# RWKV-7 / mLSTM / MoE block: dependent ScalarE and VectorE instructions a dense step apart

## The chip, the cores and the metric

The kernel runs on one core of one Trainium2 chip. The metric is the device time of one execution in microseconds. The core's engines run side by side, each in the order in which its instructions were written: TensorE (PE; its weight loads are shown as PEld), VectorE (DVE), ScalarE (ACT), GpSimd (POOL) and SyncE (SP). They wait for each other through semaphores. The order on every engine is the order in which the Python code below issues the instructions; nothing reorders them afterwards.

## What is computed

One decoder block over 256 tokens of width 2048, in float32:

```python
u = x @ w_in[i]                                    # 2048 -> RWKV-7 | mLSTM | merge gates
u_r, u_m, u_g = _split(u, [RWKV_COLS, MLSTM_COLS, GATE_COLS])
y_r = _rwkv7_mixer(u_r, ...)                       # 16 heads of 64, state updated token by token
y_m = _mlstm_mixer(u_m, ...)                       # 8 heads, chunks of 128 tokens
g_r, g_m = _split(u_g + b_gate[i], [d, d])
mix = (sigmoid(g_r) * (y_r @ w_br[i]) + sigmoid(g_m) * (y_m @ w_bm[i])) @ w_out[i]
x = _layer_norm(ALPHA * x + mix, ln1_w[i], ln1_b[i])
moe = _hier_moe(x, ...)                            # 4 groups x 8 experts, top-1 group, top-2 experts
ple = sigmoid(x @ w_pg[i]) * (p[i] @ w_ple[i])
x = _layer_norm(ALPHA * x + moe + ple, ln2_w[i], ln2_b[i])
```

In the RWKV mixer the projections are mixed with the previous token's, decay and gates come from low-rank products, and each head's output is normalised (centred, divided by its root mean square deviation), scaled, added to a bonus and gated. In the mLSTM mixer q and k pass a causal convolution of four taps and a SiLU, and each head's output is normalised and gated by a sigmoid.

## The kernel before

**The dense stage** is everything from x @ w_in to @ w_out. Its work is a list of units: a block of 256 (or 512) output columns, summed over k. `run` goes through the units in dense steps. In a step of kind "T", TensorE multiplies two k-blocks of weights with x. To keep float32 accuracy in the faster fp32r format, every weight is split into a rounded part and a rest: ScalarE copies (L217) and VectorE subtracts (L218). TensorE then does four pairs of a 512-column matmul (L282) and a 256-column one (L283). In a step of kind "N" (mLSTM's v and w_out) it does six 512-column matmuls (L290 to L292). The split of a step is issued three steps ahead (`AHEAD = 4`), into four buffers, and the loads of raw weights on SP's queue follow the splits. A unit accumulates in a pair of PSUM banks (`bank2`, two such pairs).

The steps are numbered here from 0. A w_in unit of kind "T" has 8 steps and one of kind "N" 16; a w_br or w_bm unit has 4. The order is: low-rank columns, RWKV's r, k, v in four groups of four heads mixed with the merge gates' units, q and k (`evac_qk`), v (`evac_mv`), the output gate (`evac_o`), w_br (steps 336 to 367), w_bm (to 399), w_out (to 463).

**Evacuations and mixers** fill the other engines beside the dense matmuls. Both are Python generators. After each dense step `advance` lets the first evacuation in the queue run to its next `yield`, and then the first mixer to its next one; a mixer's `yield n` lets it rest until n steps have passed. So what a generator issues between two yields stands together in one dense step, behind that step's split and dense matmuls. An evacuation starts in the last step of its unit. It begins with `total`: ScalarE copies the second half of the accumulators (L345) and VectorE adds the first (L346); then come the token shift (`shift_mix`, `shift_chunks`), the convolution (`evac_qk`) or a gate.

`rwkv(g)` is the mixer of a group of four heads. Its prologue has two table loads of ScalarE (square root L433, exponential L436) and two reciprocals (L440, L442). Then a triangular inverse in five levels, and a loop over four chunks j of 64 tokens: the state's part of the chunk is subtracted (L562 to L566), L573 multiplies with the inverse, the state is updated (L583 to L587), the output is summed (L595 to L599). `centre(tb)` takes the mean of two chunks' outputs away on VectorE (L635 to L637) and squares them on ScalarE (L638); `squares(tb)` sums the squares on VectorE (L630). In the tail come the square root (L607), reciprocal and product (L609, L611), the transposes (L615), scaling on ScalarE (L619), bonus and gate on VectorE (L621, L622), and the split of the result (L624, L625).

`mlstm` follows when the last v unit is evacuated. Its first loop has one head per round in a pipeline (`copy_out`, `finish`, `scores` in one step; `spread`, `scores_late`, `values` in the next: L784 makes what L789 multiplies). Its second loop scales two heads per step on ScalarE (L835), transposes the two before (L844), multiplies with the output gate (L848) and splits (L851, L852). `evac_br`, `evac_bm` and `evac_out` take the results of w_br, w_bm and w_out; `evac_out` adds the residual (L916), transposes (L925) and feeds the router.

**The MoE stage** streams the experts' weights (about 2 MB per load) and is not touched.

Of the kernel before, what the change touches and what calls it, by code (L numbers as in the profile page):

```python
# [116 lines left out]
def hybrid_block(ctx: ExitStack, tc: tile.TileContext, xt, xp, vec, cst, sel8, rows, ln1c, pt, w_lora, w_rkv, w_qk,  # L117
# [224 lines left out]
    def total(p_, dst=None):  # L342
# [3 lines left out]
        dve.tensor_tensor(dst, dst, p_[:, :n, :256], op=OP.add)  # L346
        return dst

    def shift_mix(dst, src, mu, omu):
        act.activation(dst, src, AF.Identity, bias=0.0, scale=omu)  # L350
        dve.scalar_tensor_tensor(dst[:, 1:], src[:, :255], mu, dst[:, 1:], op0=OP.mult, op1=OP.add)
# [28 lines left out]
    def evac_mixed(g, w):  # L380

        name, lock, old = (("mu_r", "zr", g - 1), ("mu_k", "zr", g - 1), ("mu_v", "zv", g - 2))[w]
        dst = (zr, zk, zv[:, g % 2])[w]

        def f(p_):
            t = total(p_)
            yield
            while free[lock] < old:
                yield
            for c in range(2):  # L390
                (shift_chunks if w == 2 else shift_mix)(dst[:, :, c] if w == 2 else dst[:, c], t[:, c],
                                                        *vm(name, 2 * g + c))
                yield
            if w == (1 if g else 2):
                mixers.append(rwkv(g))
        return f

    def rwkv(g):
# [159 lines left out]
        for j in range(4):  # L558
            if j:
                ps_, py = bank(), (bank(), bank())  # L560
                for c, q in quads:
                    mm(py[q][half[c], :64], PR[half[q], c, j, 1, :], S0[half[q], c, :], start=True, stop=True)  # L562
                for q, c in quads:
                    mm(ps_[half[q], 64 * c:64 * c + 64], PR[half[q], c, j, 0, :], S0[half[q], c, :], start=True,
                       stop=True)
                dve.tensor_tensor(Xs[:, :, j, :], Xs[:, :, j, :], ps_[:, :128].rearrange("p (c n) -> p c n", c=2),  # L566
                                  op=OP.add)
                for q in range(2):
                    act.activation(yN[:, j, q, :], py[q][:, :64], AF.Copy)
                yield 1  # L570
            pn = (bank(), bank())
            for c, q in quads:
                mm(pn[q][half[c], :64], Gm[half[q], j, c, :], Xs[half[q], c, j, :], start=True, stop=True)  # L573
            for q in range(2):
                act.activation(nS[:, j, q, :], pn[q][:, :64], AF.Copy, scale=-1.0)
            if 0 < j < 3:
                dve.tensor_tensor(S1, S0, scal[:, :, j:j + 1].to_broadcast([128, 2, 64]), op=OP.mult)
            yield 1
# [20 lines left out]
                dve.tensor_tensor(yN[:, j], yN[:, j], pY, op=OP.add)  # L599
            else:  # L600
                act.activation(yN[:, j], pY, AF.Copy)
            if j % 2:
                centre(j // 2)
            yield 1
            if j % 2:
                squares(j // 2)
        act.activation(rstd, rstd, AF.Sqrt, scale=1.0 / 64, bias=eps_r)  # L607
        yield 1
        dve.reciprocal(rstd, rstd)  # L609
# [8 lines left out]
        for c in range(2):  # L618
            act.activation(yT[:, c].rearrange("p (j n) -> p j n", j=4), pyc[:, c], AF.Identity,  # L619
                           scale=v_("lnx_w", 2 * g + c), bias=v_("lnx_b", 2 * g + c))  # L620
        dve.tensor_tensor(yT, yT, bon, op=OP.add)  # L621
        dve.tensor_tensor(yT, yT, gg, op=OP.mult)  # L622
        hi, lo_ = (yr[:, 2 * g:2 * g + 2, n] for n in range(2))
        act.activation(hi, yT, AF.Copy)  # L624
        dve.tensor_tensor(lo_, yT, hi.bitcast(FT), op=OP.subtract)  # L625
        free["y"] = g
        yield 1

    def squares(tb):
        dve.tensor_reduce(rstd[:, tb], ysq[:, tb], axis=AX.X, op=OP.add)  # L630

    def centre(tb):
        y = yN[:, 2 * tb:2 * tb + 2].rearrange("p j q n -> p (j q) n")
        m = mean[:, tb]
        dve.tensor_reduce(m, y, axis=AX.X, op=OP.add)  # L635
        dve.tensor_scalar(m, m, -1.0 / 64, None, op0=OP.mult)
        dve.tensor_tensor(y, y, m[:, :, None].to_broadcast([128, 4, 64]), op=OP.add)  # L637
        act.activation(ysq[:, tb], y, AF.Square)  # L638

# [27 lines left out]
    def evac_qk(u):  # L669
        w = u // 2  # L670
        dst = (qT, kT)[w]

        def f(p_):
            t = total(p_)
            yield
            while free["zr"] < 3:
                yield
            for c in range(2):
                src, i = t[:, c], 2 * u + c
                d = dst[:, i % 4]  # L680
                act.activation(d, src, AF.Identity, scale=v_("cw3", i), bias=v_("conv_b", i))
                for j in range(1, 4):
                    dve.scalar_tensor_tensor(d[:, j:], src[:, :256 - j], v_("cw%d" % (3 - j), i), d[:, j:],
                                             op0=OP.mult, op1=OP.add)
                yield
            if u % 2:
                act.activation(sgq, dst, AF.Tanh, scale=0.5)
                dve.scalar_tensor_tensor(dst, sgq, 1.0, dst, op0=OP.add, op1=OP.mult)
        return f

# [13 lines left out]

    def evac_o(u):
        def f(p_):
            t = total(p_, so[:, 2 * u:2 * u + 2])
            yield
            act.activation(t, t, AF.Tanh, scale=0.5)
            dve.tensor_scalar(t, t, 0.5, 0.5, op0=OP.mult, op1=OP.add)  # L710
            free["o"] = u
        return f

    def mlstm():
# [93 lines left out]
        for h in range(11):  # L808
# [12 lines left out]
            if 0 < h < 9:  # L821
                values(h - 1)
            if h < 9:
                yield 1
        act.activation(hrstd, hmv[:, :, :, 1], AF.Sqrt, bias=eps_m)
        dve.reciprocal(hrstd, hrstd)
        dve.scalar_tensor_tensor(hmean, hmv[:, :, :, 0], -1.0, hrstd, op0=OP.mult, op1=OP.mult)
# [3 lines left out]
        for h2 in range(5):  # L831
# [3 lines left out]
                        act.activation(hN[:, tb, h], hN[:, tb, h], AF.Identity, scale=hrstd[:, tb, h:h + 1],  # L835
                                       bias=hmean[:, tb, h:h + 1])
            if h2 == 0:
                yield 1
                continue
            h2 -= 1  # L840
            py = bank()
# [8 lines left out]
            hi, lo_ = (ym[0][:, 2 * h2:2 * h2 + 2, n] for n in range(2))  # L850
            act.activation(hi, yTm, AF.Copy)  # L851
            dve.tensor_tensor(lo_, yTm, hi.bitcast(FT), op=OP.subtract)  # L852
            yield 1

    def evac_gate(u):
        def f(p_):
            t = total(p_, gates[u // 8][:, 2 * u % 16:2 * u % 16 + 2])  # L860
            yield
            for c in range(2):
                act.activation(t[:, c], t[:, c], AF.Tanh, scale=0.5, bias=v_("b_gate", 2 * u + c))
                yield
        return f
# [3 lines left out]

    def evac_br(u):  # L870
        def f(p_):
            gt, t = gates[0][:, 2 * u:2 * u + 2], total(p_)
            yield
            dve.scalar_tensor_tensor(gt, gt, 1.0, t, op0=OP.add, op1=OP.mult)
        return f

    def evac_bm(u):
        def f(p_):
            if u == 0:
                mix.extend(_carve(big(i, FR), 0, 16, 256) for i in (4, 5))  # L880
                tmp[0] = M.rearrange("p (a t) -> p a t", t=256)[:, 0::3]
            t = total(p_)
            yield
            gr, gm = (fl(a[:, 2 * u:2 * u + 2]) for a in gates)
            dve.scalar_tensor_tensor(gates[1][:, 2 * u:2 * u + 2], gates[1][:, 2 * u:2 * u + 2], 1.0, t, op0=OP.add,
                                     op1=OP.mult)
# [1 line left out]
            yield  # L888
            hi = fl(mix[0][:, 2 * u:2 * u + 2])
            act.activation(hi, gr, AF.Copy, scale=0.5)  # L890
            dve.scalar_tensor_tensor(fl(mix[1][:, 2 * u:2 * u + 2]), gr, 0.5, hi.bitcast(FT), op0=OP.mult,
                                     op1=OP.subtract)
        return f
# [15 lines left out]
    def evac_out(u):  # L909
        def f(p_):  # L910
# [3 lines left out]
            for tb in range(2):  # L914
# [2 lines left out]
                                         op1=OP.add)  # L917
                if u < 3:
                    dve.bn_stats(stats[:, tb, u], x1[:, tb, o])
                yield  # L920
            for half in range(2):
                pz, k0 = held[1 + (2 * u + half) % 3], 4 * u + 2 * half
# [942 lines left out]
```

## Time and profile before

| | |
|---|---|
| median of three runs | 1820.55 us (1819.59 to 1824.2) |
| the profiled execution | 1823.52 us, of which the span from first to last instruction is 1821.8 |
| busy over the span | PE 1599.6 us (88%), PEld 1081.0 (59%), DVE 794.0 (44%), ACT 607.4 (33%) |
| last dense step | ends at about 851 us |
| memory traffic | 541.38 MB by DMA, 297 GB/s in the mean |

A row of the timeline holds the start and the length in us, the engine, the line, the operation, output and inputs by tile name (B, M, R, C, V, sm in SBUF, dps and mps in PSUM), shapes, and in brackets the engine's idle time before it with the instruction that ended it. Matmuls overlap, and their ends are modelled; start-to-start times are surer than busy times. A wait "X <- Y" is idle time of X's engine, ended by Y.

### The profile page before, as it was taken

Reading aid. Unit: us, or ns where it says so; the run is one execution under the profiler, and the core shown is the slowest. Engines: PE = TensorE matmul, PEld = TensorE weight load, DVE = VectorE, ACT = ScalarE, POOL = GpSimd, SP = SyncE. Lnnn points to the kernel's source line nnn. Section 1 sums busy time; section 2 is a strip of 40 time slices with the busy share of each in tenths; the row PEclk is TensorE's granted clock in tenths of the full one; section 3 lists DMA queues with packets and bytes.
Section 4 is the critical chain, followed back from the end, with each engine's and each line's share of the span. In section 5 each row is a group of like instructions: output and inputs, shape, how many; then the busy total and the mean of one; then the engine's idle time right before and its main releaser. Section 6 shows DMA issues by size and latency. Waiting matters only on the chain. (4 is left out here: it accounts for less than half of the span.)

```text
span 1821.8 us, 34784 instructions
## 1 busy us (share of the span) xinstructions
PE 1599.6 (88%) x14339; PEld 1081.0 (59%) x14339; DVE 794.0 (44%) x1664; ACT 607.4 (33%) x1179; POOL 26.6 (1%) x38
## 2 busy tenths in 40 slices
PE   7999999999989999997879787897797878987876
PEld 6787787877868778875447444455364433433332
DVE  5675756757765777854331121220211313221206
ACT  5645645646455465544111111111111111111122
POOL 0000000000000000000000000000000000000002
PEclk9999999999999999998899998899899998998888
DMA  7443434434336347975899999999999999999997
GB/s 243 157 153 116 157 129 134 151 117 141 127 105 196 106 139 240 362 228 222 353 426 427 426 425 426 393 425 426 426 426 426 426 426 396 385 427 425 426 426 323
DMA packets 68073, 541.38 MB, mean 297 GB/s; under 512 B 7740, under 2 KB 12108, under 8 KB 42016
## 3 DMA queue, kind: packets, MB, share of 16 engines
q1 hardware_dynamic: 67152, 537.33, 74.4%
q8 instruction: 142, 2.33, 0.5%
q0 software_dynamic: 720, 1.25, 0.3%
q14 instruction: 59, 0.48, 0.1%
HBM read 536.44 MB, written 2.36 MB: 296 GB/s over the span
## 5 line engine op out<-in xcount | busy, mean ns | idle before, releaser
L282 PE MATMUL dps<-B,B 128*128 128x512 f32 x1456 | 538.7, 410 | 12.1 <-ACT B L217 9.3
L283 PE MATMUL dps<-B,B 128*128 128x256 f32 x1456 | 411.0, 282 | 4.8 <-DVE B L218 4.7
L218 DVE TENSOR_TENSOR B<-B,B 128x512 fp32r<-128x512 f32 (+1 forms) x464 | 312.3, 683 | 188.9 <-ACT B L217 184.0
L1355 PE MATMUL dps<-B,B 128*32 128x256 f32 x3968 | 260.6, 418 | 87.9 <-DMA B<-in_w_gate_dram 39.9
L217 ACT ACTIVATE B<-B 128x512 fp32r<-128x512 f32 (+1 forms) x464 | 283.7, 623 | 161.8 <-PE dps L282 62.5
L282 PEld LDWEIGHTS dps<-B,B 128*128 128x128 f32 x1456 | 275.6, 189 | 84.5 <-ACT B L217 11.7
L283 PEld LDWEIGHTS dps<-B,B 128*128 128x128 f32 x1456 | 277.0, 190 | 12.3 <-DVE B L218 10.0
L1355 PEld LDWEIGHTS dps<-B,B 128*32 128x32 f32 x3968 | 139.3, 119 | 214.3 <-DMA B<-in_w_gate_dram 50.8
L1361 DVE SCALAR_TENSOR_TENSOR M<-M,dps 128x128 f32<-128x128 f32 x31 | 8.9, 289 | 401.9 <-ACT M L1360 401.9
L1719 ACT ACTIVATE B<-mps 32x512 f32<-32x512 f32 x120 | 70.6, 588 | 191.4 <-PE mps L1376 190.3
L1376 PE MATMUL mps<-B,M 128*32 128x512 f32 x992 | 127.4, 653 | 5.9 <-issue 2.7
L1170 PE MATMUL mps<-B,B 128*128 128x206 f32 (+1 forms) x640 | 112.8, 337 | 0.6 <-DVE B L1159 0.3
L1360 ACT ACTIVATE M<-dps 128x128 f32<-128x128 f32 x31 | 8.6, 278 | 309.1 <-PE dps L1355 309.1
L1170 PEld LDWEIGHTS mps<-B,B 128*128 128x128 f32 x640 | 110.6, 190 | 1.6 <-DVE B L1159 0.6
L1376 PEld LDWEIGHTS mps<-B,M 128*32 128x32 f32 x992 | 31.5, 118 | 83.5 <-issue 76.9
L290 PE MATMUL dps<-B,B 128*128 128x512 f32 x192 | 76.1, 396 | 2.7 <-ACT B L217 2.7
L292 PE MATMUL dps<-B,B 128*128 128x512 f32 x192 | 75.3, 392 | 0.9 <-DVE B L218 0.8
L291 PE MATMUL dps<-B,B 128*128 128x512 f32 x192 | 74.9, 390 | 0.0
L1427 DVE TENSOR_TENSOR B<-mps,V 128x512 f32<-128x512 f32 x31 | 21.4, 692 | 90.8 <-PE mps L1423 90.8
L1396 PE MATMUL mps<-B 128*128 128x512 f32 (+1 forms) x128 | 56.7, 595 | 0.7 <-ACT B L1719 0.7
L1183 DVE SCALAR_TENSOR_TENSOR C<-C,mps 128x412 f32<-128x412 f32 (+1 forms) x10 | 5.8, 581 | 102.6 <-PE mps L1175 102.6
L1182 ACT ACTIVATE C<-mps 128x412 f32<-128x412 f32 (+1 forms) x10 | 5.1, 512 | 129.9 <-issue 70.4
(465 smaller groups left out, 1585.0 us busy)
## 6 DMA issues: line engine op xcount, KB each, us to landing
B<-in_w_up_dram SPq DMA_DIRECT2D x62, 2048.0 KB, 24.5
B<-in_w_gate_dram SPq DMA_DIRECT2D x62, 2048.0 KB, 21.8
B<-in_w_down_dram SPq DMA_DIRECT2D x60, 2048.0 KB, 22.9
B<-in_w_gt_dram SPq DMA_DIRECT2D x64, 512.0 KB, 3.7
B<-in_w_rkv_dram SPq DMA_DIRECT2D x48, 512.0 KB, 3.9
B<-in_w_pg_dram SPq DMA_DIRECT2D x10, 1854.0 KB, 30.3
B<-in_w_out_dram SPq DMA_DIRECT2D x32, 512.0 KB, 3.7
B<-in_w_qk_dram SPq DMA_DIRECT2D x16, 512.0 KB, 4.0
```

The lines of the kernel that those rows point to most:

```text
L217: act.activation(h, src, AF.Copy)
L218: dve.tensor_tensor(wl[i % 4][:, :w], src, h.bitcast(FT), op=OP.subtract)
L282: mm(pt_[:, c], h[:, w], x.rearrange("p a t -> p (a t)"), start=k == 0, stop=False)
L283: mm(pt_[:, c, :256], l[:, w], x[:, 0], start=False, stop=k == nk - 1)
L290: mm(o, mh[:, ts_], h, start=first, stop=False)
L291: mm(o, ml[:, ts_], h, start=False, stop=False)
L292: mm(o, mh[:, ts_], l, start=False, stop=last)
L1170: mm(pp[:, tb], x1T[0][:, k, tb * 128:tb * 128 + 128], w[:, k, :n], start=k == 0 and tb == 0, stop=k == 15 and tb == 1)
L1355: mm(pu[32 * j:32 * j + 32].rearrange("p (a f) -> p a f", a=2), xs[:, 4 * q + k, :], w[:, :, k, 128 * j:128 * j + 128], start=q == QS[0] a ...
L1376: mm(pd[32 * j:32 * j + 32, :], hT_[:, 32 * c:32 * c + 32], w[:, c % 2, 512 * j:512 * j + 512], start=c == 0, stop=c == 3)
L1396: mm(pz, SWT[p0:p1, tb * 128:tb * 128 + 128], yq[p0:p1, o], start=True, stop=True)
L1719: act.activation(yq[32 * i:32 * i + 32, 512 * j:512 * j + 512], pd[32 * j:32 * j + 32, :], AF.Copy)
```

## The change

`total_slow` takes the place of `total` in all evacuations but the low-rank ones: the copy, a yield, the addition, a yield. In the other generators yields are put in wherever one of ScalarE and VectorE makes something that the other uses, or pieces are moved to a later yield. `centre` loses its last line, which becomes `square`. An mLSTM head's round takes three steps (1 + 2) instead of two, and the second mLSTM loop gives each pair of heads two steps.

```diff
+    def total_slow(p_, dst=None):
+        dst = tmp[0] if dst is None else dst
+        n = dst.shape[1]
+        act.activation(dst, p_[:, :n, 256:], AF.Copy)
+        yield
+        dve.tensor_tensor(dst, dst, p_[:, :n, :256], op=OP.add)
+        yield
+        return dst
...
         def f(p_):
-            t = total(p_)
-            yield
+            t = yield from total_slow(p_)
...
                     act.activation(yN[:, j, q, :], py[q][:, :64], AF.Copy)
+                if j == 2:
+                    centre(0)
                 yield 1
...
+            if j == 2:
+                square(0)
+            if j == 3:
+                squares(0)
...
-            if j % 2:
-                centre(j // 2)
             yield 1
-            if j % 2:
-                squares(j // 2)
+        centre(1)
+        yield 1
+        square(1)
+        yield 1
+        squares(1)
+        yield 1
         act.activation(rstd, rstd, AF.Sqrt, scale=1.0 / 64, bias=eps_r)
...
+        yield 1
         dve.tensor_tensor(yT, yT, bon, op=OP.add)
         dve.tensor_tensor(yT, yT, gg, op=OP.mult)
+        yield 1
         hi, lo_ = (yr[:, 2 * g:2 * g + 2, n] for n in range(2))
         act.activation(hi, yT, AF.Copy)
+        yield 1
         dve.tensor_tensor(lo_, yT, hi.bitcast(FT), op=OP.subtract)
...
-        act.activation(ysq[:, tb], y, AF.Square)
+
+    def square(tb):
+        act.activation(ysq[:, tb], yN[:, 2 * tb:2 * tb + 2].rearrange("p j q n -> p (j q) n"), AF.Square)
...
                 act.activation(sgq, dst, AF.Tanh, scale=0.5)
+                yield
                 dve.scalar_tensor_tensor(dst, sgq, 1.0, dst, op0=OP.add, op1=OP.mult)
...
-            t = total(p_, so[:, 2 * u:2 * u + 2])
+            t = yield from total_slow(p_, so[:, 2 * u:2 * u + 2])
+            act.activation(t, t, AF.Tanh, scale=0.5)
             yield
-            act.activation(t, t, AF.Tanh, scale=0.5)
...
             if h < 9:
-                yield 1
+                yield 2
...
             if h2 == 0:
-                yield 1
+                yield 2
...
             dve.tensor_tensor(lo_, yTm, hi.bitcast(FT), op=OP.subtract)
-            yield 1
+            yield 2
...
             hi = fl(mix[0][:, 2 * u:2 * u + 2])
             act.activation(hi, gr, AF.Copy, scale=0.5)
+            yield
...
                 if u < 3:
                     dve.bn_stats(stats[:, tb, u], x1[:, tb, o])
+                yield
+            if u < 3:
                 yield
```

Written out, the order on VectorE in the first RWKV group, from the end of chunk j = 1 (L599, after the change L613) to the wait of chunk 2 for L573's operand (L566, after it L574), is this before:

```order
L587 SCALAR_TENSOR_TENSOR B_67<-mps,B_67 128x64 x2
L599 TENSOR_TENSOR B_67<-B_67,mps 128x128
L635 TENSOR_REDUCE B_67<-B_67 128x4
L636 TENSOR_SCALAR B_67<-B_67 128x4
L637 TENSOR_TENSOR B_67<-B_67 128x256
L218 TENSOR_TENSOR B_70<-B_69,B_70 128x512
L351 SCALAR_TENSOR_TENSOR B_63<-R,V,B_63 128x255
L630 TENSOR_REDUCE B_67<-B_67 128x4
L566 TENSOR_TENSOR B_66<-B_66,mps 128x2x64
```

and after (L654 to L656 are centring, L360 the token shift's second half):

```order
L601 SCALAR_TENSOR_TENSOR B_67<-mps,B_67 128x64 x2
L613 TENSOR_TENSOR B_67<-B_67,mps 128x128
L218 TENSOR_TENSOR B_70<-B_69,B_70 128x512
L360 SCALAR_TENSOR_TENSOR B_63<-R,V,B_63 128x255
L574 TENSOR_TENSOR B_66<-B_66,mps 128x2x64
L654 TENSOR_REDUCE B_67<-B_67 128x4
L655 TENSOR_SCALAR B_67<-B_67 128x4
L656 TENSOR_TENSOR B_67<-B_67 128x256
```

Centring has moved behind the operand of L573, and the row sum L630 out of this piece.

On ScalarE, the end of the last RWKV group (L619 scaling, L624 split of the result) and the conv's gate (L687), where the v units begin, stand like this before:

```order
L681 ACTIVATE B_63<-R,V 128x256
L619 ACTIVATE B_67<-mps,V 128x256 x2
L624 ACTIVATE B_65<-B_67 128x2x256
L217 ACTIVATE B_70<-B_69 128x512
L687 ACT_TABLE_LOAD
L687 ACTIVATE B_63<-B_63 128x1024
L217 ACTIVATE B_70<-B_69 128x512 x13
```

After the change the gate (L707) stands in the chunk loop, between the state's products (L577, L585), and Square (L659) later:

```order
L701 ACTIVATE B_63<-R,V 128x256
L217 ACTIVATE B_70<-B_69 128x512
L707 ACTIVATE B_63<-B_63 128x1024
L577 ACTIVATE B_67<-mps 128x64 x2
L217 ACTIVATE B_70<-B_69 128x512
L585 ACTIVATE B_66<-mps 128x64 x2
L659 ACTIVATE B_67<-B_67 128x256
```

and the tail's end, with L635 for the scaling, L642 for the split of the result and L717 for the v unit's copy, is spread among the splits:

```order
L717 ACTIVATE B_64<-dps 128x4x128
L635 ACTIVATE B_67<-mps,V 128x256 x2
L217 ACTIVATE B_70<-B_69 128x512
L717 ACTIVATE B_64<-dps 128x4x128
L217 ACTIVATE B_70<-B_69 128x512
L642 ACTIVATE B_65<-B_67 128x2x256
L217 ACTIVATE B_70<-B_69 128x512 x14
```

The scaling and the result's copy no longer stand in one piece, and no table load follows them.

More of the change, by code (lines that the diff above doesn't have):

```diff
@@ L673, in f @@
         def f(p_):
-            t = total(p_)
-            yield
+            t = yield from total_slow(p_)
             while free["zr"] < 3:
@@ L852, in mlstm @@
             dve.tensor_tensor(lo_, yTm, hi.bitcast(FT), op=OP.subtract)
-            yield 1
+            yield 2
     def evac_gate(u):
         def f(p_):
-            t = total(p_, gates[u // 8][:, 2 * u % 16:2 * u % 16 + 2])
-            yield
+            t = yield from total_slow(p_, gates[u // 8][:, 2 * u % 16:2 * u % 16 + 2])
             for c in range(2):
@@ L871, in f @@
         def f(p_):
-            gt, t = gates[0][:, 2 * u:2 * u + 2], total(p_)
-            yield
+            gt, t = gates[0][:, 2 * u:2 * u + 2], (yield from total_slow(p_))
             dve.scalar_tensor_tensor(gt, gt, 1.0, t, op0=OP.add, op1=OP.mult)
@@ L881, in f @@
                 tmp[0] = M.rearrange("p (a t) -> p a t", t=256)[:, 0::3]
-            t = total(p_)
-            yield
+            t = yield from total_slow(p_)
             gr, gm = (fl(a[:, 2 * u:2 * u + 2]) for a in gates)
```

## Prediction

> **What bounds the kernel now.** I read the busy time on both sides of the last dense step, then TensorE's waits in the dense stage, then the timeline at each wait. First, by stretches (bounds and length in us; busy PE, PEld, DVE, ACT, POOL; granted clock, DMA share, GB/s):
>
> ```profile
> 25.00:851.00 826.00, 798.40 (x6448) 644.02 (x6446) 549.77 (x1049) 447.77 (x860) 4.51 (x12) 1.00 0.49 162
> 851.00:877.00 26.00, 17.54 (x170) 9.26 (x174) 12.28 (x67) 7.92 (x14) 0.00 (x0) 0.67 0.80 341
> 877.00:1821.00 944.00, 768.83 (x7669) 415.68 (x7661) 220.20 (x525) 140.76 (x291) 17.67 (x15) 0.92 0.98 415
> ```
>
> Up to 851 us TensorE is busy 97% of the time and the DMA engines half: the dense stage, where the whole diff lies, goes at TensorE's pace. From 877 us the DMA share is 0.98: the experts' weights stream in, and no edit touches that. The stream fills tiles that the dense stage gives back, so I let a microsecond saved before 851 move the end by a microsecond.
>
> TensorE's pace in an undisturbed step:
>
> ```profile
> 59.87 0.39 PE L282 MATMUL dps<-B,B 128*128 128x512 f32 x1
> 60.10 0.28 PE L283 MATMUL dps<-B,B 128*128 128x256 f32 x1
> 60.22 0.39 PE L282 MATMUL dps<-B,B 128*128 128x512 f32 x1
> ```
>
> A pair takes 0.35 us from start to start, a step of four pairs 1.39. ScalarE and VectorE make the split weights (L217, L218) three steps ahead; TensorE stops only when a split is later than that, or a mixer's operand is late. All its waits from 30 to 850 us (in total, times, longest):
>
> ```profile
> PE mps L573 <- DVE B L566: 5.9, 4, 2.2
> PE dps L283 <- DVE B L218: 4.7, 12, 1.1
> PE mps L615 <- DVE B L611: 4.7, 4, 1.2
> PE dps L290 <- ACT B L217: 2.7, 2, 1.8
> PE dps L282 <- ACT B L217: 1.9, 5, 0.4
> PE mps L925 <- DVE B L916: 1.9, 3, 1.0
> PE mps L789 <- DVE B L784: 1.7, 1, 1.7
> PE mps L844 <- ACT B L835: 1.1, 2, 0.7
> PE dps L292 <- DVE B L218: 0.8, 2, 0.6
> ```
>
> That is 25.4 us, and the change can win little more than this. It is not lack of speed: VectorE is busy 67% of the stage and ScalarE 54%. They stand waiting for each other while TensorE's operand lies queued behind.
>
> **The change part by part.** TensorE and VectorE get no more instructions; what moves is the step in which a dependent one is issued. The RWKV groups start 1, 7, 5 and 11 steps later, and with them go the loads of the next low-rank weights on POOL's queue, one pair a group; they are read a whole group, over 50 steps, later. SP's queue issues its loads with the splits, which stay in their steps.
>
> *Chunk loop (L573, once in each of four groups).* The first one:
>
> ```profile
> 162.38 0.42 ACT L638 ACTIVATE B<-B 128x256 f32<-128x256 f32 x1 [2.51 <-DVE B L637]
> 162.70 0.61 ACT L217 ACTIVATE B<-B 128x512 fp32r<-128x512 f32 x1
> 163.35 0.69 DVE L218 TENSOR_TENSOR B<-B,B 128x512 fp32r<-128x512 f32 x1 [1.06 <-ACT B L217]
> 164.35 0.41 DVE L630 TENSOR_REDUCE B<-B 128x4 f32<-128x256 f32 x1
> 164.68 0.28 DVE L566 TENSOR_TENSOR B<-B,mps 128x128 f32<-128x128 f32 x1
> 165.01 0.34 PE L573 MATMUL mps<-B 64*64 64x64 f32 x8 [1.18 <-DVE B L566]
> ```
>
> Square (L638) keeps ScalarE waiting 2.51 us for centring (L637); the split queued behind it is late, VectorE waits for that split, and L566, behind it and the row sum L630, is so late that TensorE stands 1.18 us. In the new order L566 stands ahead of centring, and Square comes a step after centring. Ahead of L566 VectorE then has a split (0.69) and at most one evacuation instruction as long, and both fit beside the step's 1.39 us of matmuls. All 5.9 us go. Late next is centring, 1.05 us behind L566; its reader, Square, is a step away, and the splits have their three steps. The last of these four waits cost more than itself:
>
> ```profile
> 513.80:517.20 3.40, 1.17 (x11) 0.76 (x9) 2.67 (x7) 2.35 (x7) 0.00 (x0) 1.00 0.33 65
> 517.20:520.60 3.40, 3.40 (x20) 2.56 (x24) 2.68 (x6) 1.07 (x4) 0.00 (x0) 0.50 0.23 94
> 518.39 0.63 PE L282 MATMUL dps<-B,B 128*128 128x512 f32 x1
> 519.03 0.63 PE L282 MATMUL dps<-B,B 128*128 128x512 f32 x1
> ```
>
> Behind a stretch in which TensorE worked 1.17 of 3.40 us the clock was halved for the next 3.4, and four pairs took 0.64 each instead of 0.35: 1.2 us, which I let go with the wait. [...]
>
> *Tail (L615, four times about 1.2).*
>
> ```profile
> 175.59 0.42 ACT L638 ACTIVATE B<-B 128x256 f32<-128x256 f32 x1 [2.85 <-DVE B L637]
> ```
>
> Square waits again, 2.85 us, and then the square root's table load stands ahead of the next split, so that the products (L611) reach the transposes late. The new tail has one link per step and three more steps ahead of the transposes. Some 0.12 of each 1.2 is the ordinary start of a transpose behind matmuls (my estimate from the start-to-start times), so 4.2 of the 4.7 go.
>
> *End of the last RWKV group (L290, and 0.6 of L292).*
>
> ```profile
> 539.93 0.63 ACT L624 ACTIVATE B<-B 128x512 fp32r<-128x512 f32 x1 [3.66 <-DVE B L622]
> 543.48 1.22 DVE L688 SCALAR_TENSOR_TENSOR B<-B 128x1024 f32<-128x1024 f32 x1 [1.60 <-ACT B L687]
> ```
>
> ScalarE waits 3.66 us for the mixer's last products with the splits behind it; the conv's gate (L687, L688) follows. After the change the products, their copy and the difference stand in steps 288 to 290, a step each, and L687 and L688 long before, in 275 and 276, with no load. Each stop of a split's matmul costs 0.16 more than its gap (below), so 2.7 + 0.6 + 3 x 0.16 = 3.8.
>
> *mLSTM (L789, L844).*
>
> ```profile
> 641.47 0.46 PE L789 MATMUL mps<-B,B 128*128 128x129 f32 x2 [1.73 <-DVE B L784]
> 657.12 0.81 PE L844 MATMUL mps<-C,B 128*128 128x128 f32 x4
> L844 PE MATMUL mps<-C,B 128*128 128x128 f32 x16 | 4.7, 315 | 1.6 <-ACT B L835 1.1
> ```
>
> L844's four groups take 4.7 busy and 1.6 idle; at 0.81 each they would take 3.2, so 3.1 is lost, to scalings of ScalarE that come one by one. With L789: 4.8. The third step gives both two steps of cover instead of one. It adds no TensorE work; mLSTM's last transposes move from dense step 340 to 350, and w_br runs to 367, so matmuls still cover them.
>
> *Prologues and small waits (L282, L283, the rest of L292).*
>
> ```profile
> 79.72 0.63 ACT L217 ACTIVATE B<-B 128x512 fp32r<-128x512 f32 x1 [0.75 <-PE dps L282]
> 81.22 0.60 ACT L345 ACTIVATE R<-dps 128x512 f32<-128x512 f32 x1 [0.87 <-PE dps L283]
> 81.84 1.28 ACT L433 ACT_TABLE_LOAD   x1
> 83.13 0.60 ACT L433 ACTIVATE B<-mps 128x512 f32<-128x512 f32 x1
> 88.29 1.75 DVE L440 RECIPROCAL B<-B 128x256 f32<-128x256 f32 x1
> 89.18 0.39 PE L282 MATMUL dps<-B,B 128*128 128x512 f32 x1
> 90.64 0.39 PE L283 MATMUL dps<-B,B 128*128 128x256 f32 x1 [1.06 <-DVE B L218]
> ```
>
> The last two rows are 1.46 apart instead of 0.23: 1.23 lost where the gap says 1.06, hence the 0.16. The rows hold 4.7 + 1.9 + 0.2 in 18 stops, with 0.16 each 9.7. Most of it is the four prologues: the copy L345 waits for a unit's end, and a table load stands behind it. The mixer shifts against the units, so in the first group the load directly follows L217 (80.4 instead of 81.8, 1.4 earlier). But the two reciprocals of 1.75 remain, and in the second and third group an evacuation's addition of 0.69 now comes just ahead of one. Between nothing and all 9.7 I take 40%, 3.8: two groups win about 1, two less, and the small waits of w_bm half of theirs.
>
> *w_out (L925).* The added step removes the longest wait, 1.0; the other 0.9 is at the last unit, where nothing changes.
>
> Sum: 5.9 + 1.2 + 4.2 + 3.8 + 4.8 + 3.8 + 1.0 = 24.7. Each tail and prologue now meets other evacuations than before; for these eight places I charge 0.2 each, 1.6, between nothing and a 1.2 as at L573: 23.1.
>
> *Table loads* go from 36 to 34 in the written order, off the path. One new load precedes mLSTM's first exponential, where ScalarE idled:
>
> ```profile
> 584.26 0.21 ACT L729 ACTIVATE sm<-sm 128x16 f32<-128x16 f32 x1 [1.47 <-DVE sm L728]
> ```
>
> 1.47 covers a load of 1.28, at no cost. [...]
>
> The profiled execution took 1823.5 (its span of 1821.8 and 1.7 around it), 3.0 over the median of the three runs, 1820.55. 1823.5 - 23.1 - 3.0 = 1797.4; I say **1797**.
>
> **The rivals.**
> *Half of it comes back.* Waits move instead of vanishing: 11.5 us gained, 1809. For it: the reciprocals that stay, and the new neighbours of each tail. Against: the largest terms each hang on one named instruction that no longer stands in front.
> *No change: the experts' stream starts no earlier*, 1820. For it: from 851 to 877 us the clock is 0.67 and could fall worse. Against: the DMA share there is 0.80, less than later, so the stream waits for tiles.
> *Slower: the accumulators are held longer.* TensorE has two PSUM pairs for the dense units, and VectorE's addition frees one a step later than before. It would bite where units are shortest, in w_br and w_bm:
>
> ```profile
> 702.00:747.00 45.00, 44.45 (x247) 37.61 (x247) 37.62 (x59) 24.72 (x45) 0.00 (x0) 1.00 0.81 292
> ```
>
> A w_bm unit is four steps, 5.56 us, and VectorE's eight instructions in it take at most 8 x 0.69 = 5.5. Above 5.56 the lag would grow until TensorE waits for the pair. The whole is slower from 1.8 us in each of the 16 units ((23.1 + 5.5) / 16); at 2.2 it is 1832. Against: 37.62 of 45 is 84%.
>
> **How the numbers follow.** Chances: my sum, 17 to 31 us gained, 0.76; half, 0.15; no change, 0.05; slower, 0.04. Low end: all of the 9.7 and of L925 and no charge, 23.1 + 5.9 + 0.9 + 1.6 = 31.5, 1789. High end: the half, 1809. About 0.3%, 5.5 us, is what a measurement tells from no change: faster 0.89 (the first two, less 0.02 of the half), same 0.07, slower 0.04.
>
> **What would show it.** Right: TensorE waits for L574 (now L566's line) are gone; the transposes L631 wait no more than 0.3; no wait in the mLSTM values' steps behind the last group; L865 in groups of 0.8; a clock of 1.00 from 25 us to the last dense step, which ends near 828; and behind it 971 us as now, within 5. Wrong: over 8 us of waits left in the prologues, TensorE waiting for the addition (now L354), or a longer part behind the dense stage.

## The result, and the profile after

The changed kernel took 1800.73 us (median of four runs, 1798.97 to 1804.28), the kernel before 1821.48 (median of four): a ratio of 0.9882, 95% interval 0.9867 to 0.9896, or 18.9 to 24.2 us less. The prediction was 1797. The profiled execution took 1798.97 us, its span 1797.3. It is the shortest of the four.

The stretches again (columns as before), cut at the last dense step and 26 us later:

```profile
25.00:828.00 803.00, 792.99 (x6453) 643.73 (x6451) 546.03 (x1050) 444.09 (x858) 4.50 (x12) 1.00 0.50 167
828.00:854.00 26.00, 17.55 (x170) 9.10 (x173) 12.11 (x66) 7.82 (x14) 0.00 (x0) 0.67 0.81 346
854.00:1797.00 943.00, 769.27 (x7669) 417.12 (x7661) 220.17 (x525) 140.61 (x291) 17.66 (x15) 0.92 0.99 416
```

TensorE does the same matmuls in 803 us instead of 826, busy for 793 of them. The part behind is as it was: the DMA share is 0.99, before 0.98. What TensorE still waits for from 30 us to 828 (in total, times, longest); the lines of the change have moved down by 8 to 21, so that L551 is a matmul of the five levels that build the inverse, L810 was L789, L946 was L925 and L1148 the router's L1127:

```profile
PE dps L283 <- DVE B L218: 4.9, 10, 1.1
PE mps L946 <- DVE B L935: 0.9, 2, 0.8
PE mps L551 <- DVE B L546: 0.8, 1, 0.8
PE dps L282 <- ACT B L217: 0.7, 2, 0.4
PE mps L1148 <- ACT R L1140: 0.7, 1, 0.7
PE mps L810 <- DVE B L805: 0.7, 1, 0.7
PE dps L292 <- DVE B L218: 0.7, 1, 0.7
```

These rows hold 9.4 us, where the list before held 25.4. The chunk loop (L573, now L583), the tail's transposes (L615, now L631), L290 and mLSTM's last transposes (L844, now L865) are gone from the list. Two rows are new or worse: L551, and nearly half of the L283 row, which now lies in mLSTM's second loop and in w_bm. (L1148's wait is not new: it was 1.13 before, at 850.83, just outside the window of that list.) The chunk loop of the first group, around the matmul that stood 1.18 us at 165.01 and now follows without a wait:

```profile
163.99 0.29 DVE L574 TENSOR_TENSOR B<-B,mps 128x128 f32<-128x128 f32 x1 [0.62 <-PE mps L572]
164.20 0.41 DVE L654 TENSOR_REDUCE B<-B 128x4 f32<-128x256 f32 x1
...
164.85 0.43 DVE L656 TENSOR_TENSOR B<-B 128x256 f32<-128x256 f32 x1
...
165.49 0.34 PE L583 MATMUL mps<-B 64*64 64x64 f32 x8
```

VectorE stands 0.62 us waiting for TensorE there, where TensorE had waited for VectorE, and centring (L654 to L656) comes behind the operand. The same matmul of the last group, behind which the clock had been halved, is at 520.06 now, and the stretch behind it runs at the full clock:

```profile
520.06:523.46 3.40, 3.40 (x50) 2.64 (x50) 3.35 (x8) 1.80 (x5) 0.00 (x0) 1.00 0.52 153
```

To measure the dense stage alone I take the time from a matmul of the first group to the last dense matmul. Both rows for the kernel before, then for the changed one:

```profile
76.00 1.02 PE L419 MATMUL mps<-B,C 128*128 128x512 f32 x2
845.26 0.39 PE L292 MATMUL dps<-B,B 128*128 128x512 f32 x1
```

```profile
78.86 1.02 PE L427 MATMUL mps<-B,C 128*128 128x512 f32 x2
822.55 0.39 PE L292 MATMUL dps<-B,B 128*128 128x512 f32 x1
```

The first of each pair stands a dense step (1.39 us) later in the changed order, so before is 845.26 - 77.39 = 767.9 and after 743.7: **24.2 us** shorter. The last dense step itself moved by 22.7 only, because this execution reached the first group 1.5 us later in its start-up.

### The profile page after: what moved, and what is told of

It reads as the page before. It is cut to its first block, busy times and chain, and to the rows that moved or that the text cites. A ratio compares the mean times of both kernels' runs of the same rounds, so it can differ in the third digit from the quotient of the medians.

```text
span 1797.3 us, 34835 instructions
## 1 busy us (share of the span) xinstructions
PE 1594.4 (89%) x14339; PEld 1081.7 (60%) x14339; DVE 789.8 (44%) x1664; ACT 603.4 (34%) x1177; POOL 26.6 (1%) x38
## 3 DMA queue, kind: packets, MB, share of 16 engines
q0 software_dynamic: 720, 1.25, 0.3%
## 5 line engine op out<-in xcount | busy, mean ns | idle before, releaser
L282 PE MATMUL dps<-B,B 128*128 128x512 f32 x1456 | 535.9, 408 | 11.2 <-ACT B L217 8.1
L283 PE MATMUL dps<-B,B 128*128 128x256 f32 x1456 | 410.9, 282 | 5.0 <-DVE B L218 4.9
L282 PEld LDWEIGHTS dps<-B,B 128*128 128x128 f32 x1456 | 275.1, 189 | 82.4 <-ACT B L217 9.8
L1376 PE MATMUL dps<-B,B 128*32 128x256 f32 x3968 | 254.0, 412 | 71.0 <-DMA B<-in_w_up_dram 33.1
L283 PEld LDWEIGHTS dps<-B,B 128*128 128x128 f32 x1456 | 276.7, 190 | 12.2 <-DVE B L218 10.1
L290 PE MATMUL dps<-B,B 128*128 128x512 f32 x192 | 77.1, 402 | 0.0
L1417 PE MATMUL mps<-B 128*128 128x512 f32 (+1 forms) x128 | 62.5, 645 | 1.3 <-ACT B L1740 0.7
```

Source lines behind the costliest of these rows:

```text
L282: mm(pt_[:, c], h[:, w], x.rearrange("p a t -> p (a t)"), start=k == 0, stop=False)
L283: mm(pt_[:, c, :256], l[:, w], x[:, 0], start=False, stop=k == nk - 1)
L290: mm(o, mh[:, ts_], h, start=first, stop=False)
L1376: mm(pu[32 * j:32 * j + 32].rearrange("p (a f) -> p a f", a=2), xs[:, 4 * q + k, :], w[:, :, k, 128 * j:128 * j + 128], start=q == QS[0] a ...
L1417: mm(pz, SWT[p0:p1, tb * 128:tb * 128 + 128], yq[p0:p1, o], start=True, stop=True)
```

## The experiments

Twelve kernels ran, each timed in five rounds against the kernel before. "Stage" is the length just defined; what part of it is a wait for a tile of w_out, a transfer, stands apart, the half clock behind it included (0.50 for 3.41 us in u_end and u_total; a_hook is about that). Stops behind a late tile of w_bm, at most 1.5 us (u_total), are not set apart.

| kernel | ratio to before (95%) | stage, us | of it w_out's tile |
|---|---|---|---|
| before | 1 | 767.9 | 0 |
| b_end | 0.9998 (0.9988 to 1.0009) | 767.3 | 0 |
| b_shift | 0.9965 (0.9954 to 0.9977) | 763.9 | 0 |
| b_chunk | 0.9959 (0.9943 to 0.9975) | 760.3 | 0 |
| delays | 0.9943 (0.9925 to 0.9961) | 757.5 | 0 |
| u_tail | 0.9888 (0.9867 to 0.9910) | 749.2 | 1.4 |
| u_end | 0.9885 (0.9867 to 0.9902) | 749.7 | 3.9 |
| u_chunk | 0.9887 (0.9868 to 0.9906) | 748.4 | 0.5 |
| a_shift | 0.9869 (0.9855 to 0.9884) | 747.0 | 1.4 |
| u_total | 0.9854 (0.9830 to 0.9877) | 746.7 | 3.1 |
| u_mlstm | 0.9871 (0.9853 to 0.9889) | 746.0 | 2.0 |
| after | 0.9882 (0.9867 to 0.9896) | 743.7 | 0 |
| a_hook | 0.9871 (0.9854 to 0.9887) | 743.8 | 0 |
| imp_all | 0.9820 (0.9802 to 0.9838) | 735.3 | 0 |

The times of the kernels near the changed one can't be told apart by their intervals; the waits in the traces can. In most kernels the stage's gain passes to the time one for one as far as the intervals tell: delays 10.4 us of stage and 0.0057 x 1826 = 10.4 of time, b_chunk 7.6 and 7.5, imp_all 32.6 and 32.9. In b_shift and u_total the time won more (6.4 and 26.7) than the stage (4.0 and 21.2): their profiled executions, 1824.8 and 1804.62, were the slowest of their kernels, 5.4 and 7.3 over the medians. Each stage is one profile.

A difference of about 1 us between two stages says nothing about an edit. The changed kernel and a_hook have the same instructions on every engine but for the place of one load. The same 36 dense steps of w_br and w_bm, first in the one and then in the other:

```profile
664.64:714.56 49.92, 49.92 (x290) 44.02 (x289) 38.68 (x63) 27.77 (x48) 0.00 (x0) 1.00 0.80 283
```

```profile
663.58:714.46 50.88, 50.88 (x290) 44.10 (x289) 38.77 (x62) 27.82 (x48) 0.00 (x0) 1.00 0.80 279
```

TensorE is never idle and the clock is full in both, yet a step takes 1.387 us in the one and 1.413 in the other. Over the first 25 of these steps the kernel before, delays and u_chunk go at the slower pace too, the other kernels at the faster; the cause is open. About 1 us of the 24.2 is this pace and not the change.

**One part put back at a time.**

*u_chunk*: the chunk loop's norm as before, in the changed kernel.

```
-                if j == 2: centre(0)
...
-            if j == 2: square(0)
-            if j == 3: squares(0)
...
+            if j == 1:
+                centre(0); square(0)
             yield 1
+            if j == 1: squares(0)
```

> The changed kernel with the chunk loop alone put back: centring and Square of the first two chunks in the step of their last product, the row sum a step later. No step is added or taken away, so every group meets the same units. My theory (each part's own wait returns, and passes to the end one for one): TensorE waits for the chunk loop's VectorE addition again in each of the four groups, 5.9 us in all, and if one of the four is as long as the 2.2 of before, the clock is halved behind it (1.2 more): 6 to 7 us slower than the changed kernel, about 0.992 of the kernel before. Rival (the gain came from where the groups now stand against the dense units, not from what is spaced): under 2 us slower, 0.989.

Its waits for the chunk loop (L581 here):

```profile
PE mps L581 <- DVE B L574: 1.7, 2, 1.1
```

1.7 us in two groups, the longest 1.1, not 5.9 in four. Without the wait for w_out's tile the stage is 4.2 longer than the changed kernel's; 0.9 of the remainder are two stops in w_bm, where ScalarE waited 2.89 us for a tile (1.20 in the changed kernel), 0.7 is the slower pace there and in w_br, and for the rest no stop is long enough to name. Neither theory holds: in the changed kernel's places the old order waits, but in two groups of four.

*u_tail*: the tail's norm together again.

```
+            if j == 3:
+                centre(1); square(1)
             yield 1
-        centre(1); yield 1; square(1); yield 1
         squares(1)
-        yield 1
         act.activation(rstd, rstd, AF.Sqrt, ...)
...
         free["y"] = g
-        yield 1
+        yield 4
```

> The changed kernel with the tail's norm alone put back: centring and Square of the last two chunks together, the row sum and the square root together; the three steps that this saves stand at the group's end, so that the next group starts where it did. My theory: the transposes of the tail wait for the products again, about 1 us in each group: 4 us slower than the changed kernel, 0.9905 of the kernel before. Rival (where the groups stand is what counts): under 1.5 us.

```profile
PE mps L629 <- DVE B L625: 3.8, 4, 1.7
```

3.8 idle in four stops, 4.1 in the stage: as my theory had it.

*u_end*: the three steps at the end of a group taken out.

```
-        yield 1
         dve.tensor_tensor(yT, yT, bon, op=OP.add)
         dve.tensor_tensor(yT, yT, gg, op=OP.mult)
-        yield 1
         hi, lo_ = ...
         act.activation(hi, yT, AF.Copy)
-        yield 1
         dve.tensor_tensor(lo_, ...)
         free["y"] = g
-        yield 1
+        yield 4
```

> The changed kernel with the last products, their copy and the difference of a group in one step again, the three steps put at the group's end. My theory as predicted: ScalarE waits for the products with the splits behind it, at the end of the last group 3.8 us, in the first three groups nothing: 3.8 slower than the changed kernel, 0.990 of the kernel before. Rival (the loss of before was that this step met the conv's gate, which the later start of the last group already keeps away from it): under 1 us.

At the last group's end one stop of 0.2 us came back; the first three ends lost 0.3, 0.3 and 0.8, and the stage 2.1 in all. The predicted 3.8 did not hang on these three steps.

*u_mlstm*: two steps for an mLSTM head, at the three places of the diff.

```
-                yield 2
+                yield 1
```

> The changed kernel with two steps for an mLSTM head again instead of three; everything else as changed. By the prediction 4.8 us slower than the changed kernel (0.991 of the kernel before). By the trace of the changed kernel, where the second mLSTM loop has new waits for the splits of about 3 us, only 1 to 2 us slower (0.989): the wait had moved from the transposes to the splits. No gain from the third step at all is the other end.

```profile
PE mps L810 <- DVE B L805: 1.4, 1, 1.4
PE mps L865 <- ACT B L856: 0.5, 1, 0.5
```

These waits are back, but those for the splits at 641 to 661 us are down to one pair. Over the steps that hold mLSTM the two kernels take the same time (100.6 us each); the 0.3 by which the stage without w_out's tile is longer lies behind them. The third step moved the wait. The timeline of the changed kernel says how:

```profile
653.23 0.62 ACT L217 ACTIVATE B<-B 128x512 fp32r<-128x512 f32 x1
...
653.75 1.64 ACT L856 ACTIVATE B<-B,B 128x128 f32<-128x128 f32 x4
...
655.98 0.63 ACT L872 ACTIVATE B<-B 128x512 fp32r<-128x512 f32 x1 [0.60 <-DVE B L869]
...
656.52 1.14 ACT L217 ACTIVATE B<-B 128x512 fp32r<-128x512 f32 x2
...
658.00 0.39 PE L283 MATMUL dps<-B,B 128*128 128x256 f32 x1 [0.30 <-DVE B L218]
```

A pair of heads gives ScalarE four scalings (L856, 1.64) and then a copy (L872) that waits for VectorE, all in one step. Between two splits lie 3.29 us, more than two dense steps, and the matmuls of the next splits stop. From 641 to 662 us eight stops for splits cost 3.8 us from start to start, where the kernel before lost 0.9: that gave back most of what L865 and L810 won. Four of the eight stand behind scalings (1.7 us); two stand behind the square root ahead of the scalings, a table load and 2.12 us of waiting for VectorE (1.1), and two behind the last copy (1.1), as in the kernel before.

**The later starts alone.** *delays* is the kernel before with these lines, the first in the evacuations of the RWKV, conv and w_bm units.

```
             t = total(p_)
             yield
+            yield
...
         free["y"] = g
-        yield 1
+        yield 7
```

> The kernel before with the later starts alone: each RWKV evacuation ends a step later and six steps stand at each group's end, so that all four groups start in the very steps of the changed kernel; nothing is spaced inside them, and mLSTM is as before. My theory (spacing is what removes the waits): the waits of the chunk loop (5.9 us), of the tail (4.7) and of the prologues stay, only the end of the last group may lose its 3.8, as the run with the last products put back showed no wait there: 0 to 4 us faster than the kernel before, ratio 0.998 to 1.0. Rival (where the groups stand against the dense units is what counts): most of the 20.8 us is won, at least 12, ratio 0.9935 or less. With the chunk loop put back only 1.9 of its 5.9 us came back, which is for the rival; the rest is a middle, 5 to 12.

```profile
PE dps L283 <- DVE B L218: 4.3, 8, 1.6
PE mps L574 <- DVE B L567: 3.6, 3, 2.5
PE mps L616 <- DVE B L612: 2.9, 4, 1.1
PE dps L282 <- ACT B L217: 0.2, 1, 0.2
```

The stage is 10.4 us shorter, the middle. Nothing was spaced, and yet the chunk loop's 5.9 fell to 3.6, the tail's 4.7 to 2.9, ScalarE's late splits (L282) from 1.9 to 0.2, and the 3.8 at the last group's end are gone. My theory as I had put it falls. Up to the end of the conv the later starts alone win 12.4 of the changed kernel's 21.0 us; mLSTM, whose code is as before, lost 1.7 of that here, with a wait of 2.0 and a half clock behind it (0.50 for 3.42 us). So the place of a group against the units is worth about as much as the spacing. What the spacing alone is worth in the old places is known for two parts only, by the next kernel and by b_end.

**The chunk loop alone, in the old places.** *b_chunk* is the kernel before with these lines.

```
+                if j == 2: centre(0)
                 yield 1
...
+            if j == 2: square(0)
+            if j == 3: squares(0)
...
-            if j % 2: centre(j // 2)
+            if j == 3: centre(1); square(1)
             yield 1
-            if j % 2: squares(j // 2)
+            if j == 3: squares(1)
```

> The kernel before with the chunk loop's norm alone spaced (centring of the first two chunks behind VectorE's addition of the third, Square a step later, the row sum two), every group in the steps of before. My theory: the four waits of TensorE for that addition go, 5.9 us, and with the 2.2 among them the halved clock behind it, 1.2 more: 7 us faster than the kernel before, ratio 0.996. Rival for the clock (the wait alone did not halve it): the halved stretch stays, 5.9. Rival (spacing helps only together with the later start): under 3 us.

The wait for the chunk loop is absent from its list; the stage is 7.6 us shorter, against 5.9 + 1.2 predicted for this term. There is a half clock in this kernel too, 0.50 for 3.41 us behind the end of the last group (TensorE waits 1.8 us up to 536.7):

```profile
533.68:537.10 3.42, 1.63 (x8) 0.94 (x6) 2.63 (x5) 1.63 (x3) 0.00 (x0) 1.00 0.01 2
537.10:540.51 3.41, 3.41 (x8) 1.67 (x6) 1.82 (x3) 3.40 (x6) 0.00 (x0) 0.50 0.53 151
```

**The addition back in its old step.** *u_total*, in the changed kernel's `total_slow`:

```
         act.activation(dst, p_[:, :n, 256:], AF.Copy)
-        yield
         dve.tensor_tensor(dst, dst, p_[:, :n, :256], op=OP.add)
         yield
+        yield
```

> The changed kernel with VectorE's addition of each evacuation in the same step as ScalarE's copy again, the step that this saves put behind it, so that all later steps stay. My theory: the prologues' waits for the splits come back in part, 2 to 4 us over the dense stage, and the small waits of w_bm with them. Rival (the later step cost as much at w_bm and the last prologues as it won at the first): within 1 us of the changed kernel.

The rival: 743.6 without w_out's tile, as the changed kernel. The prologues wait 0.6 less, the conv 0.3 and mLSTM 1.9 less, a tail 0.4 more, w_bm 1.4 more behind a tile that came late (ScalarE waits 3.06 us for it, 1.20 in the changed kernel), and stops too short to name make up the rest. By this one profile, the one part of the change that touches every unit wins nothing by itself.

**Place or spacing.** *b_end* has the three steps of a group's end in the kernel before, for the last group alone, so that nothing else moves.

```
+        if g == 3: yield 1      (ahead of the products, of the copy, of the difference)
```

> The kernel before with the last products, their copy and the difference a step apart in the last RWKV group alone; no group starts elsewhere. In the changed kernel with this end put back the wait did not return, and in the kernel with the later starts alone it was gone too, so the later start is enough to remove it. Theory one (either is enough: the wait needs this end and the conv's gate in the same steps): the 3.8 us of the splits' matmuls go here as well, ratio 0.998. Theory two (only the start removes it): within 1 us of the kernel before.

Theory two: the waits stay (0.8 and 1.9 idle). The timelines of ScalarE and VectorE show why:

```profile
538.69 1.52 DVE L689 SCALAR_TENSOR_TENSOR B<-R,V,B 128x255 f32<-128x255 f32 x3
...
540.29 1.28 ACT L693 ACT_TABLE_LOAD   x1 [1.79 <-DVE B L689]
541.58 1.06 ACT L693 ACTIVATE B<-B 128x1024 f32<-128x1024 f32 x1
...
542.67 1.23 DVE L694 SCALAR_TENSOR_TENSOR B<-B 128x1024 f32<-128x1024 f32 x1 [1.86 <-ACT B L693]
...
545.88 0.50 PE L292 MATMUL dps<-B,B 128*128 128x512 f32 x1 [1.94 <-DVE B L218]
```

It is the conv's evacuation that holds both engines: ScalarE waits 1.79 for its products and loads a table, VectorE waits 1.86 for its tanh, and the splits stand behind. The later start of the group keeps its own end away from this.

*b_shift*, in the kernel before:

```
         free["y"] = g
-        yield 1
+        yield 4
```

> The kernel before with three steps more at each RWKV group's end and nothing else: by the written order the second and the fourth group then start three steps later and the first and the third where they did. Theory one (a group's place against the dense units decides its waits): the waits of the first and third group stay as before, to 0.3 us each, those of the second and fourth change, by something between 2 and 8 us in all. Theory two (the gain of the later starts came from the evacuations that end a step later): all four groups wait as before, under 1.5 us in all.

Theory one. The first and third group wait 1.25 for the chunk loop and 1.06 for the tail, as before. The second and fourth wait nothing for the chunk loop, where they had lost 1.4 and 2.3; but the fourth's tail now meets the conv's gate (L687, L688):

```profile
536.01 1.06 ACT L687 ACTIVATE B<-B 128x1024 f32<-128x1024 f32 x1
...
537.10 1.23 DVE L688 SCALAR_TENSOR_TENSOR B<-B 128x1024 f32<-128x1024 f32 x1 [1.67 <-ACT B L687]
...
539.31 1.09 PE L615 MATMUL mps<-C,B 128*128 128x128 f32 x4 [5.71 <-DVE B L611]
```

This is the longest wait of TensorE in the dense stage of any run, 5.71 us, where before it was 1.1 and with six steps more (delays) 0.7. Where an unspaced part falls is a matter of luck.

*a_shift*, in the changed kernel:

```
         free["y"] = g
-        yield 1
+        yield 2
```

> The changed kernel with one step more at each group's end: the second, third and fourth group start 1, 2 and 3 steps later than in the changed kernel. Theory one (what is spaced no longer depends on the place): TensorE waits in the groups within 1.5 us in all of the changed kernel's. Theory two (the changed kernel sits at a lucky place): 3 us or more of waits come back in the chunk loop, the tail and the prologues.

Between the two, nearer the first: the chunk loop waits nothing in any group, the tail 1.0 in all, and the prologues, which the change leaves unspaced, wait 0.9 more; 1.9 in the stage without w_out's tile. What is spaced waits little in the new places (the chunk loop nothing, the tail at most 0.6 at once); what is not spaced changes again.

**A transfer that is now only just in time.** At about 752 us TensorE stopped 1.4 to 2.4 us in u_tail, u_end, u_mlstm, u_total and a_shift, 0.5 in u_chunk, and in the changed kernel not at all. ScalarE's rows, of the changed kernel and of u_end:

```profile
749.90 1.15 ACT L217 ACTIVATE B<-B 128x512 fp32r<-128x512 f32 x2 [4.19 <-DMA B<-in_w_out_dram]
```

```profile
752.29 1.15 ACT L217 ACTIVATE B<-B 128x512 fp32r<-128x512 f32 x2 [5.12 <-DMA B<-in_w_out_dram]
```

The split waits for a tile of w_out. The split is made three steps (4.2 us) ahead; here a wait of 4.19 cost nothing and one of 5.12 did. Over the 20 us ahead of it the DMA share is 0.95 to 0.99. *a_hook* moves one of the experts' loads that share the queue.

```
-HOOK_W = (-10, -5, 1, 7, 17)
+HOOK_W = (-10, -5, 1, 10, 17)
```

> The changed kernel with the third of the experts' loads that go ahead between w_out's tiles three tiles later; no engine's instruction moves. In the four kernels of the first set ScalarE waited 4.7 to 5.1 us for a tile of w_out where the stage of w_bm ends, and TensorE 0.5 to 2.4 behind it; in the changed kernel's own profile 4.2 and nothing. Theory one (the experts' load in front of w_out's tiles makes them late): ScalarE's longest wait for a tile there falls below 3.5 and TensorE waits for none; total 0 to 2 us less than the changed kernel. Theory two (the queue is full there anyway): ScalarE waits as long as before, at this tile or three later.

Its ScalarE, in the list of waits from 725 to 790 us:

```profile
ACT B L217 <- DMA B<-in_w_out_dram: 1.7, 1, 1.7
```

Theory one: from 4.2 to 1.7, and TensorE does not stop. It is one profile, and the changed kernel's own had no stop either; the time is not to be told from the changed kernel's. imp_all, which has the same load later, still has one wait of 4.0 for a tile of w_out, at 733.8.

**The rule carried further.** *imp_all* spaces what the changed kernel left, and has the load of a_hook. Its main edits:

```
-        dve.reciprocal(ss[:, 0], ss[:, 0]); yield 2; dve.reciprocal(ss[:, 1], ss[:, 1]); yield 2
+        four reciprocals of 128 columns, yield 1 behind each
...
+            if h2 < 3: scale(2 * h2 + 3)      (mLSTM: two scalings a step, three steps for two heads)
...
+                    if j == 2: yield          (conv: the third product a step later)
...
-    ((5, 6, fold b), (7, 6, fold w), (8, 3, fold_sums))
+    ((5, 4, product b), (6, 4, sum b), (7, 4, product w), (8, 4, sum w), (8, 7, fold_sums))
```

> The changed kernel with the same rule carried further at the waits that it left: mLSTM's scalings two to a step, with three steps for a pair of heads; the folding of the router's weights in four steps where VectorE has least instead of two; the two reciprocals of 1.75 us as four of half the columns, one a step; the conv's three products of an evacuation in two steps; and the third of the experts' loads that go ahead between w_out's tiles three tiles later. From the changed kernel's waits: mLSTM's second loop 3.8 us, w_bm 1.9, the prologues 3.6, the conv 0.9, and the wait for w_out's tile 0 to 2. My theory: half or more of the 10.2 goes, dense stage 5 to 8 us shorter, ratio to the kernel before about 0.985. Rival (the time is at its floor, what is spaced here meets something else): within 2 us of the changed kernel, 0.988.

```profile
PE dps L283 <- DVE B L218: 2.0, 6, 0.8
PE mps L958 <- DVE B L947: 0.9, 2, 0.8
PE mps L814 <- DVE B L809: 0.7, 1, 0.7
PE dps L282 <- ACT B L217: 0.4, 1, 0.4
```

The L283 row falls from 4.9 to 2.0, L551's wait and the splits' stops behind the scalings of pairs of heads are gone, and the prologues wait 1.0 instead of 3.6. The stage is 8.4 us shorter. 1793.09 us median (1790.8 to 1797.2), a ratio of 0.9820: it beats both kernels, since its interval ends at 0.9838 where the changed kernel's begins at 0.9867 (the two were measured in different sets, each against the kernel before).

## Why the prediction was right, and which of its steps were not

The sum was 24.7 less a charge of 1.6, so 23.1; the stage is 24.2 shorter, the router's wait 0.4 less, and the measured time 18.9 to 24.2 less. The parts, by start-to-start times at each place:

- *Chunk loop, 5.9 and the half clock 1.2*: right, and shown: b_chunk, which has this edit alone, wins 7.6. The working left out that the later starts by themselves would have taken 2.3 of the 5.9 (and 1.8 of the tail's 4.7).
- *Tail, 4.2*: right in size (u_tail gives back 4.1).
- *End of the last group, 3.8*: right in size, wrong in cause. The step that failed is "after the change the products, their copy and the difference stand in steps 288 to 290, a step each". b_end has that and wins nothing. The half-sentence behind it, that L687 and L688 now stand long before, is what counts: delays has only that, and loses 0.2.
- *mLSTM, 4.8*: mis-sized: the steps that hold it are 1.9 us shorter (102.57 and 100.64), 0.4 of that by the pace, so it won 1.5, and the third step by itself, by u_mlstm, nothing. That "the third step gives both two steps of cover" holds for the transposes; of L789's 1.7, 0.7 is left, against the sign that none would be. The working did not ask what the new order does to the splits, which stand behind the scalings and the square root on ScalarE; their stops grew by 2.9.
- *Prologues and small waits, 3.8 of 9.7*: too low for the prologues, 4.7 (8.3 became 3.6), too high for w_bm, which lost about 0.6 instead of winning: the folding of the router's weights (0.75 and 1.20 on VectorE) meets a heavier step than before. And the prologues' gain came with the place: delays, which spaces nothing, has them at about 2.5.
- *w_out, 1.0*: 1.1.
- *The charge, 1.6*: 0.9 of it came, at the levels' matmul L551 behind the conv's products, and nothing in the tails.

The errors of mLSTM (3.3 too high) and the prologues (1 to 2 too low), the pace (about 1) and stops too short to list cancelled: the sum was better than its parts, and that is luck. The start-up, 1.5 us later in the profile of after than in that of before, is in no term. One for one behind the last dense step held: from the router's first matmul (850.83 and 827.68) to the end it took 971.0 before and 969.6 after, and 968 to 975 over all the kernels run, with no trend against the stage's length that this scatter would show.

The rivals: "half of it comes back" did happen, to mLSTM alone. "The accumulators are held longer" did not: no row of TensorE waits for the addition, in any of the kernels. The two table loads fewer (ScalarE's instructions went from 1179 to 1177) are off the path, as said.

## What to carry to other kernels

Where two engines with queues in order make operands for each other and for a third, give every hand-over a step of its own: in the places tried here the spaced chunk loop cost TensorE nothing and the four spaced tails 1.0 us in all at most (a_shift), while a single unspaced one cost anything from 0 to 5.7 us with each shift of a few steps. A gain that comes with a shift belongs to the place, so test the shift alone before the edit is credited. And ask what a spaced chain puts in one step of its own: four scalings and a copy in one step cost the splits behind them 1.7 us of the about 3 that the transposes had won.

## What the runs showed of the hardware

*The clock was halved behind some waits and not behind others.* In delays a wait of 2.5 us left it at 1.00, and behind one of 2.0 it was 0.50 for 3.42 us. The first two rows hold the 2.5 us of the chunk loop, the last two the 2.0 of mLSTM, 100 us later:

```profile
521.13:524.54 3.41, 2.21 (x23) 1.51 (x22) 2.02 (x5) 2.38 (x6) 0.00 (x0) 1.00 0.21 84
524.54:527.95 3.41, 2.07 (x26) 1.47 (x30) 2.78 (x6) 1.44 (x5) 0.00 (x0) 1.00 0.18 26
...
626.94:630.35 3.41, 1.43 (x11) 1.10 (x10) 3.27 (x11) 1.66 (x4) 0.00 (x0) 1.00 0.37 127
630.35:633.77 3.42, 3.42 (x13) 2.94 (x12) 2.00 (x8) 1.98 (x4) 0.00 (x0) 0.50 0.36 81
```

Of other stretches of 3.41 to 3.42 us, those with 1.63 us of matmuls (b_chunk, from 533.68) and 1.88 (u_total, 750.84) had a clock of 0.50 behind them, and those with 2.04 (u_mlstm, 751.52) and 2.20 (a_shift, 751.02) one of 1.00. But it was 1.00 behind 1.64 (the kernel before, 537.68) and 0.50 behind 2.41 (the changed kernel, 855.94, past the dense stage): what decides it was not shown. So the predicted 1.2 us was partly luck too: it went by one wait of 2.2 us, and the longer one of delays cost no clock.

*A split three steps ahead covered 4.2 us of a late transfer*: a wait of 4.19 cost TensorE nothing, one of 4.67 cost 0.5, and five of 5.03 to 5.12 cost 1.4 to 2.4, the more, the longer ScalarE had waited for an earlier tile of w_out (1.8 to 3.0 us). The faster stage has used up this margin.
